# Five plain MLP pairs per layer take their weights' low parts from adding transfers, and a thirteenth pair per layer takes seven products

## The chip, the core and the metric

The kernel runs on one core of a Trainium2 chip. The core has TensorE (PE in the profile; its weight loads, which run beside its matmuls, are PEld), VectorE (DVE), ScalarE (ACT), GpSimd (POOL) and SyncE (SP), and 16 DMA engines that move data between HBM and SBUF. Each engine runs its own instructions in a fixed order and waits at semaphores for the others. The metric is the time of one execution on the device, in microseconds (us).

## The reference, cut to what matters

A decoder trunk of two layers in float32, on 512 positions of width 1024. Each layer has a mixer, a cross-attention into 256 memory tokens, and a gated MLP. The change is in the MLP:

```python
def conv_ffn(h, w_up, w_conv, w_down):
    u = causal_dwconv(h @ w_up, w_conv)
    gate, val = jnp.split(u, 2, axis=-1)
    return (jax.nn.silu(gate) * val) @ w_down
...
for l in range(DEPTH):
    ...
    x = x + conv_ffn(rmsnorm(x, norm_ffn[l]), ffn_w_up[l], ffn_conv[l], ffn_w_down[l])
```

`w_up` is 1024 x 5632 and `w_down` 2816 x 1024, so a layer has 22 pairs of 128-wide columns of `w_up`: gate column block j and value block 22+j.

## The kernel before

**Two parts per operand.** Each float32 operand is carried as two parts in TensorE's reduced float32 type: `hi`, the rounded value, and `lo`, what is left of it. A product is three matmuls: hi with hi, hi with lo, lo with hi (L484). Activations lie transposed, with features on partitions and the 512 positions as columns.

**Weights.** All weights lie in HBM as `wts`, in slots of 128 x 1024 float32 (512 KB). SP loads slot after slot into a ring of three buffers, `raw` (the function `loads`). The function `prep` makes `hi` by a cast on ACT (L431) and `lo` by a subtraction raw - hi on DVE (L446), each in a ring of five buffers, and then frees the raw buffer. A plain up-projection pair has two slots (four of the eight k blocks each) and 8 x 2 x 3 = 48 matmuls of 512 columns, in `lin_stream`.

**Pairs with seven products.** The pairs in the table `SEVEN` take another way, with matrices halved in each direction (2 x 2 blocks) and seven block products in place of eight. `prep_halved` takes the two slots as four blocks of 128 x 512, splits the first slot ("a") and one block ("d") as they are, makes sums and differences of the blocks in place (four DVE operations of 128 x 512), and splits these two slots ("b" and "c"). `lin_halved` runs the products, each four k steps of three matmuls 256 wide, and puts them together by seven additions 256 wide on DVE. What the products read of the activations is made once per layer by `fold`: scaled rows (`N["S"]`, tiles `y` and `h`) and their differences and sums (`N["T"]`, tiles `kl`, `pt`, `so`, `rrow`), four steps of two feature blocks; a product waits for the step that it reads. Before, pairs 8 to 11, 13 and 15 to 21 are in the table, in both layers.

**Order in the MLP.** `FFN_ORDER` sets it: up-projections 0 to 7, then the first part of the down-projection (columns in four pieces, `d 0 0` to `d 0 3`) with pairs 8 to 10 between the pieces, then pairs 11 to 16, the second part with 17 to 20 between, pair 21, and the rest of the down-projection. The MLP's norm runs beside the first pairs: sums of squares (`nacc`, `sq`) are turned by PE, reduced by DVE, POOL takes the power -1/2 (tile `k`, L446, from `s` and `mhalf`), PE spreads that over the partitions (`tr<-ident,k`, L488), and ACT copies it into the tile `rrow`. Pairs 0 to 5 run on unscaled rows `hs`, and their results are multiplied by `rrow` afterwards; pairs 6 and 7 and all later ones read rows that are scaled already.

**What sets the order.** No engine's order is written by hand. Streams of operations (loads, preparation, each matmul stream, each epilogue) ask the class `Issue` for buffers and for their turn. It keeps a modelled time for every engine, takes the operation that can start first, and among those within a small tolerance the one of lowest priority number. So a change in one stream's operations or modelled times can move others. The chip then runs each engine's list in that order, whatever the true times are.

## Time and profile before

| | |
|---|---|
| runs, median (lowest to highest) of 3 | 1478.06 us (1477.45 to 1478.25) |
| the profiled execution, its time | 1477.59 us |
| its span | 1475.8 us |
| granted clock of TensorE, mean | 1.00 |
| PE busy | 1469.9 us, 7832 matmuls |
| weight loads busy | 1265.6 us |
| DVE busy | 1165.7 us (79% of the span) |
| ACT busy | 784.1 us (53%) |
| POOL busy | 65.9 us (4%) |
| read from HBM | 142.92 MB |

The profile is taken from one execution. Its time contains its span and a little around it. A row of the costliest groups reads: line, engine, operation, output and inputs by the program's names with their tile sizes, how often, then busy time, the mean of one in ns, and the idle time just before them with what ended most of it. A row of the trace by time reads: start, length, engine, line, operation. The arrow `<-` behind a wait names the engine, tile and line whose work ended it. The clock is 1.00 throughout, so a matmul's time is the same in every stage.

### The profile page before, as it was taken

What the parts mean: (1) busy time and instruction counts of PE and PEld (TensorE: products, weight loads), DVE (VectorE), ACT (ScalarE), POOL (GpSimd) and SP (SyncE); (2) the same over time, 40 slices, a digit from 0 to 9 for tenths busy, and PEclk for the clock granted to TensorE, in tenths of its full rate; (3) what the DMA queues carried; (4) which work ended last, traced back from release to release, by engine and by line L of the source; (5) the groups of instructions that cost most, each with busy time, mean ns of one, the idle gap of its engine ahead of it and who ended that gap; (6) DMA issues with size and microseconds to landing.
All of it is one profiled execution on the core that took longest, in us unless ns stands there. A gap on an engine that the chain in (4) does not pass through costs nothing.

```text
span 1475.8 us, 20602 instructions
## 1 busy us (share of the span) xinstructions
PE 1469.9 (100%) x7832; PEld 1265.6 (86%) x7832; DVE 1165.7 (79%) x1953; ACT 784.1 (53%) x1297; POOL 65.9 (4%) x139
## 2 busy tenths in 40 slices
PE   9999999999999999999999999999999999999998
PEld 8888888888888899999888888888888889989897
DVE  7689767665898888988688989867657998788883
ACT  6576446453654445445477877755435654354441
POOL 3210000000000000000100000000000000000000
PEclk9999999999999999999999999999999999999999
DMA  6122435311232221324221121451212222323232
GB/s 237 58 86 72 138 134 173 113 58 58 100 107 94 98 93 68 114 98 139 94 72 58 58 100 58 143 171 66 86 64 101 100 75 100 112 86 104 96 113 74
DMA packets 42721, 146.33 MB, mean 99 GB/s; under 512 B 4864, under 2 KB 5376, under 8 KB 42624
## 3 DMA queue, kind: packets, MB, share of 16 engines
q1 hardware_dynamic: 42624, 145.04, 28.8%
q8 instruction: 61, 1.00, 0.3%
q14 instruction: 36, 0.29, 0.1%
HBM read 142.92 MB, written 2.10 MB: 98 GB/s over the span
## 4 chain that ended last, share of the span: by engine, by line
PE 96%; DVE 2%; ACT 1%; issue 0%; DVEq 0%; POOL 0%; POOLq 0%
PE acc L484 72%; PE sc L484 11%; PE pv L484 6%; PE tr L484 5%; PE tr L488 3%; ACT h L431 0%; DVE lo L446 0%; ACT g L434 0%; DVE h L446 0%; DVE c L446 0%; DVE g L446 0%; DVE g L1545 0%; DVE kl L454 0%; ACT pt L431 0%; DVE pt L446 0%
## 5 line engine op out<-in xcount | busy, mean ns | idle before, releaser
L484 PE MATMUL acc<-hs,hi 128*128 128x512 f32 x1568 | 495.2, 392 | 0.0
L431 ACT CAST hi<-raw 128x1024 fp32r<-128x1024 f32 (+1 forms) x288 | 297.4, 1039 | 220.2 <-PE acc L484 81.2
L446 DVE TENSOR_TENSOR lo<-raw,hi 128x1024 fp32r<-128x1024 f32 (+1 forms) x288 | 345.4, 1206 | 67.0 <-ACT hi L431 64.6
L484 PEld LDWEIGHTS acc<-hs,hi 128*128 128x128 f32 x1568 | 292.8, 188 | 57.7
L484 PE MATMUL acc<-hs,lo 128*128 128x512 f32 x784 | 307.0, 392 | 0.0
L484 PE MATMUL acc<-h,hi 128*128 128x512 f32 (+1 forms) x672 | 195.6, 375 | 0.0
L484 PE MATMUL acc<-hi,hs 128*128 128x512 f32 x544 | 176.2, 395 | 0.0
L484 PEld LDWEIGHTS acc<-hs,lo 128*128 128x128 f32 x784 | 147.3, 188 | 28.6
L484 PEld LDWEIGHTS acc<-h,hi 128*128 128x128 f32 x672 | 122.4, 188 | 22.4 <-DVE x L446 0.6
L446 DVE TENSOR_TENSOR x<-x,acc 128x512 f32<-128x512 f32 (+1 forms) x105 | 70.9, 680 | 71.3 <-PE acc L484 71.0
L484 PE MATMUL acc<-h,lo 128*128 128x512 f32 (+1 forms) x336 | 124.8, 374 | 0.0
L484 PEld LDWEIGHTS acc<-hi,hs 128*128 128x128 f32 x544 | 101.3, 188 | 19.8 <-ACT hs L434 0.2
L484 PE MATMUL acc<-lo,hs 128*128 128x512 f32 x272 | 106.4, 392 | 0.0
L454 DVE SCALAR_TENSOR_TENSOR g<-c,pp,g 128x510 f32<-128x510 f32 (+1 forms) x144 | 101.5, 747 | 0.9 <-ACT g L434 0.9
L484 PE MATMUL acc<-y,hi 128*128 128x512 f32 (+1 forms) x352 | 99.2, 363 | 0.0
L484 PEld LDWEIGHTS acc<-h,lo 128*128 128x128 f32 x336 | 63.3, 188 | 11.3
L484 PEld LDWEIGHTS acc<-y,hi 128*128 128x128 f32 x352 | 63.6, 189 | 10.6
L446 DVE TENSOR_TENSOR g<-g,g 128x512 f32<-128x512 f32 (+2 forms) x112 | 62.9, 569 | 4.2 <-ACT g L434 1.7
L434 ACT ACTIVATE g<-c,pp 128x512 f32<-128x512 f32 x72 | 49.5, 719 | 30.4 <-DVE c L446 30.2
L434 ACT ACTIVATE g<-sc,rq 128x128 f32<-128x128 f32 (+7 forms) x128 | 62.0, 540 | 3.6 <-PE sc L484 3.3
L484 PE MATMUL acc<-y,lo 128*128 128x512 f32 (+1 forms) x176 | 63.7, 362 | 0.0
L431 ACT CAST pt<-tr 128x128 fp32r<-128x128 f32 (+2 forms) x96 | 43.0, 456 | 31.1 <-PE tr L488 30.6
(238 smaller groups left out, 2432.4 us busy)
## 6 DMA issues: line engine op xcount, KB each, us to landing
raw<-wts SPq DMA_DIRECT2D x256, 512.0 KB, 3.7
x<-xT SPq DMA_DIRECT2D x16, 256.0 KB, 5.4
raw<-wts SPq DMA_DIRECT2D x8, 256.0 KB, 5.3
raw<-memT SPq DMA_DIRECT2D x4, 512.0 KB, 4.4
outT<-x SPq DMA_DIRECT2D x7, 256.0 KB, 2.0
outT<-x SPq DMA_DIRECT2D x2, 128.0 KB, 1.7
pp<-par SPq DMA_DIRECT2D x1, 175.5 KB, 4.9
sq<-par SPq DMA_DIRECT2D x1, 128.0 KB, 5.1
```

The source lines that it names most:

```text
L431: return nc.scalar.copy(out=out.ap, in_=in_.ap)
L434: return nc.scalar.activation(out=out.ap, in_=in_.ap, func=func, scale=_raw(scale), **kw)
L446: lambda: _ve(eng).tensor_tensor(out=out.ap, in0=in0.ap, in1=in1.ap, op=op))
L454: lambda: nc.vector.scalar_tensor_tensor(out=out.ap, in0=in0.ap, scalar=_raw(scalar), in1=in1.ap, op0=op0, op1=op1))
L484: lambda: nc.tensor.matmul(out.ap, lhsT.ap, rhs.ap, start=start, stop=stop))
L488: return Op("PE", 0.109, [in_, ident_v], [out], lambda: nc.tensor.transpose(out.ap, in_.ap, ident_v.ap))
```

## The change

Three edits go together.

1. **A thirteenth pair with seven products.** Pair 7 joins the table `SEVEN` in both layers. It was the last plain pair ahead of the first down-projection; it now runs 84 matmuls 256 wide in place of 48 that are 512 wide.
2. **Low parts by adding transfers.** For pairs 2 to 6 of both layers (the set `LOW`, two slots each, 20 slots in all) DVE's subtraction goes. ACT writes minus the rounded raw value into `lo` (an ACTIVATE with scale -1), and a transfer that POOL issues adds the slot from HBM onto it: `lo` = wts - hi. The planner takes 1.0 us of POOL for the issue and counts the result as there 10 us later (`land`).
3. **Another layout and other signs in the halved pairs.** Their four blocks are stored one behind the other in HBM, in the order a11, a21, a22, a12 by block row and column, and a load takes two of them (rows of 2 KB in place of 4 KB). Some of the sums change sign: three of the four operations in `prep_halved` become additions, and three of the additions in `lin_halved` become subtractions.

The file also gains a path in which sums of blocks are made in HBM (`sums_in_dram`, `SUMMED`, `ADDED`, `LOW7`); its tables are empty, so nothing of it runs. `FFN_ORDER` is written out with the same content.

```diff
-SEVEN = {l: (8, 9, 10, 11, 13, 15, 16, 17, 18, 19, 20, 21) for l in range(2)}
+SEVEN = {0: (7, 8, 9, 10, 11, 13, 15, 16, 17, 18, 19, 20, 21), 1: (7, 8, 9, 10, 11, 13, 15, 16, 17, 18, 19, 20, 21)}
+
+SUMMED = {0: {}, 1: {}}
...
+LOW = {GN[n] for n in ('U2_0', 'U2_1', 'U3_0', 'U3_1', 'U4_0', 'U4_1', 'U5_0', 'U5_1', 'U6_0', 'U6_1')}
+LOW7 = {GN[n] for n in ()}
...
             self.free_at[op.eng] = end
+            end += op.land
...
+    def add_dma(out, in_):
+
+        out = vw(out)
+        i = in_.ap if isinstance(in_, V) else in_
+        o = Op("POOL", 1.0, [out] + [x for x in (in_,) if isinstance(x, V)], [out],
+               lambda: nc.gpsimd.dma_start(out=out.ap, in_=i, accum_op=ALU.add, max_dma_last_dim=2048))
+        o.land = 10.0
+        return o
...
+    def blocks(gi):
+
+        return wts[FIRST[gi]:FIRST[gi] + 2].rearrange("s p c -> (s p c)").rearrange("(b p c) -> b p c", b=4, p=P)
...
+    def halved_loads(gi):
+        x = blocks(gi)
+        take = [("a", x[0:4:3]), ("r", x[1:3])]
...
+        for n, src in take:
+            w = 512 if n == "d" else SLOT
+            raw = yield AL(pRAW, F32, (P, w), parts=w // 512)
+            v = raw.v().re("p (b c) -> p b c", c=512)
+            src = src.re("b p c -> p b c") if isinstance(src, V) else src.rearrange("b p c -> p b c")
+            yield dma(v, src, w)
+            raws[gi, n] = raw
...
     def prep_halved(gi):
...
-        yield tt(a11, a11, a21, ALU.subtract)
+        yield tt(a11, a11, a21, ALU.add)
         yield tt(a21, a21, a22, ALU.add)
-        yield tt(a22, a22, a11, ALU.subtract)
-        yield tt(a12, a12, a22, ALU.subtract)
+        yield tt(a22, a22, a11, ALU.add)
+        yield tt(a12, a12, a22, ALU.add)
...
                     yield act(hi, raw)
-                    yield tt(lo, raw, hi.v().f32(), ALU.subtract)
+                    if gi in LOW:
+                        yield act(lo, raw, scale=-1.0)
+                        yield add_dma(lo, wts[FIRST[gi] + s])
+                    else:
+                        yield tt(lo, raw, hi.v().f32(), ALU.subtract)
                     prepped[gi, s, 0] = prepped[gi, s, 1] = (hi, lo)
                 free(raw)
...
+        def sub(out, a, ps):
+            return tt(out, a, ps[:, :256], ALU.subtract)
+
+        def neg(out, a, ps):
+            return tt(out, ps[:, :256], a, ALU.subtract)
...
-        then(Until(lambda: "p1" in st), add(c12, c11, p6), lambda: free(p6), flag("p6"),
+        then(Until(lambda: "p1" in st), sub(c12, c11, p6), lambda: free(p6), flag("p6"),
...
-             add(c12, c12, p5), flag("p5"), add(c22, c21, p5), lambda: free(p5),
-             add(c21, c21, p4), lambda: free(p4), lambda: done(1, u2))
+             sub(c12, c12, p5), flag("p5"), neg(c22, c21, p5), lambda: free(p5),
+             neg(c21, c21, p4), lambda: free(p4), lambda: done(1, u2))
```

Lines behind the edits shift by 8 (up to 17 further on): DVE's and POOL's L446 is L454 after, ACT's L431 and L434 are L439 and L442, PE's L484 is L492, the new transfer is L508.

What the edits do to the order shows at three places of the first layer; the second layer has the same at its own. On POOL, around the power that gives the MLP norm, this stood before (the rows with `mhalf` are powers; the third is that of the MLP norm):

```order
L446 TENSOR_TENSOR k_3078<-s_3113,mhalf 128x4
L446 TENSOR_TENSOR k_3223<-s_3273,mhalf 128x4
L446 TENSOR_TENSOR k_3722<-s_3743,mhalf 128x4
L446 TENSOR_TENSOR k_7008<-s_7025,mhalf 128x4
L497 MEMSET g_7056 128x512
```

And this after, at the same place:

```order
L454 TENSOR_TENSOR k_3080<-s_3115,mhalf 128x4
L454 TENSOR_TENSOR k_3225<-s_3275,mhalf 128x4
L508 DMA lo_3689<-wts 128x2x512
L508 DMA lo_3716<-wts 128x2x512
L454 TENSOR_TENSOR k_3723<-s_3743,mhalf 128x4
L508 DMA lo_3747<-wts 128x2x512
L508 DMA lo_3826<-wts 128x2x512
L508 DMA lo_3859<-wts 128x2x512
```

Two of the layer's ten adding transfers (pair 2's two slots) stand ahead of the power on POOL, eight behind it. On ACT, from the copy of the norm's row on, as pairs 0 to 2 end (`hi` casts of raw slots, `y` and `h` casts for the fold, `g` activations of the pairs' results), this stood before:

```order
L431 COPY rrow_3768<-tr_3753 128x512
L434 ACTIVATE g_3787<-c_3692,pp 128x512
L434 ACTIVATE g_3793<-c_3738,pp 128x512
L434 ACTIVATE g_3805<-c_3797,pp 128x512
L431 CAST hi_3819<-raw_3703 128x1024
L434 ACT_TABLE_LOAD
L434 ACTIVATE g_3787<-g_3787 128x512
L431 CAST y_3836<-c_3780 128x512
L431 CAST h_3842<-g_3793 128x512
```

And this after, where `lo_3826` and `lo_3859` are the copies for pair 3's second and pair 4's first slot:

```order
L439 CAST hi_3825<-raw_3717 128x1024
L442 ACT_TABLE_LOAD
L442 ACTIVATE g_3791<-g_3791 128x512
L439 CAST y_3840<-c_3784 128x512
L442 ACTIVATE lo_3826<-raw_3717 128x1024
L439 CAST h_3848<-g_3797 128x512
L439 CAST hi_3858<-raw_3738 128x1024
L442 ACTIVATE g_3809<-g_3809 128x512
L442 ACTIVATE g_3863<-c_3850,pp 128x512
L439 CAST y_3875<-c_3785 128x512
L442 ACTIVATE lo_3859<-raw_3738 128x1024
```

Each cast of a `hi` is followed, some rows later, by the new copy into `lo` from the same raw buffer, with rows of the fold and of the epilogues between them. The third place is the end of the fold on DVE, with pair 7 beside it. Before, from the last four sums of the fold (`c`) on to its last two low parts (`pt_3777` and `rrow_3779`):

```order
L446 TENSOR_TENSOR c_4256<-c_4256 128x256
L446 TENSOR_TENSOR c_4256<-c_4257,c_4256 128x256
L446 TENSOR_TENSOR c_4257<-c_4257,c_4256 128x256
L446 TENSOR_TENSOR c_4257<-c_4257 128x256
L446 TENSOR_TENSOR pt_3777<-c_4256,pt_3777 128x512
L454 SCALAR_TENSOR_TENSOR g_4311<-acc_4130,pp,g_4311 128x511
L446 TENSOR_TENSOR rrow_3779<-c_4257,pt_3777 128x512
```

And the rows from the second of those sums on after, where `raw_4045` and `raw_4084` are pair 7's two loads:

```order
L454 TENSOR_TENSOR c_4187<-c_4188,c_4187 128x256
L454 TENSOR_TENSOR raw_4045<-raw_4045,raw_4084 128x512
L462 SCALAR_TENSOR_TENSOR g_4242<-c_4235,pp,g_4242 128x511
L454 TENSOR_TENSOR c_4188<-c_4188,c_4187 128x256
L454 TENSOR_TENSOR raw_4084<-raw_4084 128x512
L462 SCALAR_TENSOR_TENSOR g_4242<-c_4235,pp,g_4242 128x510
L454 TENSOR_TENSOR c_4188<-c_4188 128x256
L454 TENSOR_TENSOR pt_3781<-c_4187,pt_3781 128x512
L454 TENSOR_TENSOR g_4242<-g_4242,g_4197 128x512
L454 TENSOR_TENSOR raw_4084<-raw_4084,raw_4045 128x512
L462 SCALAR_TENSOR_TENSOR g_4275<-acc_4153,pp,g_4275 128x511
```

Three of pair 7's four sums now stand among the last steps of the fold; its last low part (`rrow_3783`) comes three rows further on, ahead of the fourth sum. On PE, pair 7's seven products stand where its wide matmuls stood, ahead of the first down-projection, and the rows outside the MLPs keep their order but for single matmuls of the norms.

## The prediction

> **What bounds the kernel now.** I read the page first, for the chain that ended last and TensorE's (PE's) share of it.

> ```profile
> span 1475.8 us, 20602 instructions
> ...
> PE 96%; DVE 2%; ACT 1%; issue 0%; DVEq 0%; POOL 0%; POOLq 0%
> ```

> PE carries 96% of the chain. What VectorE (DVE) or ScalarE (ACT) save counts only where PE waits for them, so the waits by engine come second; for PE they are these, in the whole run.

> ```profile
> PE pv L484 <- POOL pt L497: 1.1, 1, 1.1
> PE sc L484 <- DVE s L1022: 0.4, 1, 0.4
> PE sc L484 <- ACT g L434: 0.3, 1, 0.3
> ```

> None lies in the MLPs. The windows third: the plain up-projections of the first MLP, the rest of it, and the second MLP's plain part.

> ```profile
> 389.00:474.00 85.00, 85.00 (x382) 70.59 (x381) 80.72 (x123) 47.49 (x67) 0.00 (x0) 1.00 0.26 89
> ...
> 475.00:738.00 263.00, 263.00 (x1630) 237.73 (x1630) 216.11 (x327) 120.65 (x160) 4.32 (x11) 1.00 0.30 101
> ...
> 1133.00:1218.00 85.00, 85.00 (x379) 70.34 (x378) 79.48 (x121) 46.83 (x67) 0.94 (x1) 1.00 0.26 88
> ```

> The columns are the stretch, its length, then busy time of PE, weight loads, DVE, ACT and GpSimd (POOL). PE is busy all the time at clock 1.00; DVE is near full in the plain parts (80.7 of 85 us) and hides behind PE. So the MLPs cost what PE's matmuls cost at their pitch, and a busy DVE costs nothing yet.

> **PE's own work.** The chain in order of time (start, length, what) gives the pitch.

> ```profile
> 344.91 39.44 PE acc L484 x174
> ...
> 474.25 1.44 PE sc L484 x12
> 475.69 1.44 PE pv L484 x12
> ```

> The first row is 512-wide matmuls alone: 39.44/174 = 226.7 ns each. The others are one product of a seven-product pair each: 12 matmuls, 256 wide, 120.0 ns each. Pair 7 in each layer leaves 2 column blocks x 8 k x 3 = 48 wide matmuls, 10.88 us, for 7 x 12 = 84 narrow ones, 10.08 us. That saves 0.80 us a pair, **1.60 us** in both layers. Everything else that PE runs stays the same.

> [...]

> **DVE and ACT.** These groups hold the kinds of operation that change; the last two figures ahead of the idle time are busy us and mean ns of one.

> ```profile
> L446 DVE TENSOR_TENSOR lo<-raw,hi 128x1024 fp32r<-128x1024 f32 x280 | 339.9, 1221 | 61.1 <-ACT hi L431 58.8
> ...
> L431 ACT CAST hi<-raw 128x1024 fp32r<-128x1024 f32 x280 | 292.5, 1052 | 217.2 <-PE acc L484 81.2 <-DVE raw L446 62.3 <-DMA raw<-wts 56.5
> ...
> L446 DVE TENSOR_TENSOR raw<-raw,raw 128x512 f32<-128x512 f32 x72 | 49.5, 687 | 0.6
> ...
> L446 DVE TENSOR_TENSOR c<-c,sc 128x256 f32<-128x256 f32 x96 | 37.1, 416 | 0.2
> ```

> Ten low parts of a layer leave DVE: 10 x 1.22 = 12.2 us. Pair 7 gives up two (2.4 us) and takes three whole ones, a half-size one and four sums at 0.69, and seven 256-wide additions at 0.42: 3.7 + 3.4 + 2.9 = 10.0 us. DVE nets about 4.6 us less a layer. The negated copy on ACT isn't in the trace; I take the cast of its size, so ACT gains 10 x 1.05 = 10.5 us a layer, and some 2 for pair 7, on 47.5 busy in 85. Bounds for a changed sign or a swapped operand are the rows themselves, which hold adds and subtractions of one size. All of this lies beside PE, so I cost it at nothing.

> What pair 7 could uncover is the fold: its products read the folded activations, which are finished last here.

> ```profile
> 454.30 0.68 DVE L446 TENSOR_TENSOR rrow<-c,pt 128x512 fp32r<-128x512 f32 x1
> ...
> L446 DVE TENSOR_TENSOR lo<-raw,hi 128x1024 fp32r<-128x1024 f32 x11 | 13.5, 1230 | 0.0
> ...
> 461.78 0.61 PE L484 MATMUL acc<-h,hi 128*128 128x512 f32 x2
> ```

> The middle row counts low parts from 389.2 to 455. By the new order one of that size, a half-size one and three sums of pair 7 are left ahead of the last fold: 10 x 1.23 go, 4 x 0.69 come, and the fold ends some 9 us earlier, near 445. The last row is the first down-projection, so pair 7 takes PE's 10.88 us ahead of it, from 450.9, and its third product ends its reads of the fold at 455. The cover is about 9 us; without it PE would wait for what is missing of it.

> **The halved pairs' loads** stay 512 KB each, in rows half as long.

> ```profile
> raw<-wts SPq DMA_DIRECT2D x256, 512.0 KB, 3.7
> ...
> DMA to landing us min/median/max: 3.3/3.7/6.1
> ...
> 465.82 1.22 DVE L446 TENSOR_TENSOR lo<-raw,hi 128x1024 fp32r<-128x1024 f32 x1
> ...
> 477.21 0.28 PE L484 MATMUL tr<-kl,lo 128*128 128x256 f32 x1
> ```

> The bounds are 3.3 and 6.1 us to landing, so a load can come 2.4 us later or 0.4 earlier; the last two rows show such a pair's low part made 10 us before PE reads it. Cost nothing; without that cover, up to 2.4 us a pair.

> **The adding transfers.** Two questions: how long POOL is held, and when the sum has landed.

> POOL first. The new order puts two transfers ahead of the power that gives the MLP's norm.

> ```profile
> 381.90 1.05 ACT L431 CAST hi<-raw 128x1024 fp32r<-128x1024 f32 x1 [0.90 <-PE acc L484]
> ...
> 385.81 1.01 POOL L446 TENSOR_TENSOR k<-s,mhalf 128x4 f32<-128x4 f32 x1 [59.48 <-DVE s L464]
> 388.08 0.60 PE L488 MATMUL tr<-ident,k 128*128 128x128 f32 x4
> ...
> L493 SPq DMA_DIRECT2D raw<-wts x264: 327/328/714, 1.2 to 1439.2; - x132
> ...
> L446 POOL TENSOR_TENSOR s<-s,mhalf 128x8 f32<-128x8 f32 x8 | 14.1, 1758 | 55.8 <-DVE s L469 35.0 <-DVE s L464 19.0 <-DVE s L446 1.7
> ```

> The second transfer waits for cast and copy of pair 2's second half: 381.90 + 2 x 1.05, so POOL issues it at about 384.2. PE transposes the power's result at 388.08, one matmul earlier in the new order, 387.85; the power takes 1.01 us, so it must start by 386.8. Behind it queue PE's transposes, ACT's row copy and DVE's first scalings, which free PE's accumulators. An issue may hold POOL for up to 2.6 us before PE waits. Bounds for one: 0.33 us (SyncE's) and 1.76 us (POOL's longest row); I take 1.0, the power's own. No wait at either end.

> [...]

> Then the landing. Of the ten low parts the tightest is the second of pair 3, the next the second of pair 4.

> ```profile
> 393.75 1.06 ACT L431 CAST hi<-raw 128x1024 fp32r<-128x1024 f32 x1 [1.04 <-PE acc L484]
> ...
> 396.66 0.60 ACT L431 CAST y<-c 128x512 fp32r<-128x512 f32 x1
> ...
> 404.77 1.05 ACT L431 CAST hi<-raw 128x1024 fp32r<-128x1024 f32 x1
> ...
> 410.55 0.39 PE L484 MATMUL acc<-hs,lo 128*128 128x512 f32 x1
> ...
> 421.43 0.39 PE L484 MATMUL acc<-hs,lo 128*128 128x512 f32 x1
> ```

> Pair 3's copy stands behind the cast at 396.66 in ACT's new order (its high part is cast at 393.75) and ends at about 397.25 + 1.0 = 398.3; PE reads it at 410.55: 12.3 us. Pair 4's cast is at 404.77, one 0.6 us cast and the copy follow, to 407.5; PE reads at 421.43: 13.9 us. Bounds for issue and landing: 3.3 us, the quickest load, and 2 x 6.1 + 1.76 = 14.0, since what lies there is read as well as what is added. I take 2 x 3.7 + 1.0 = 8.4, nearest the median load: nothing waits. At 14.0 PE waits 1.7 + 0.1 us a layer, 3.6 in all. What hides the transfers is the ring of five buffers; without it each would cost its 8.4 us.

> **The sum.** -1.60 on PE, and nothing else. The profiled execution took 1477.59 us, its span and 1.8 around it: 1475.99. It stands 0.47 below the median of the runs, 1478.06, so I forecast **1476.4**.

> **The rivals.**
> - Slower: the sums land late. It decides where landing takes over 12.3 us; from 13.1 it has eaten the gain (2 x 0.8). With four median loads' time and the issue, 15.8 us, PE waits 3.5 and 1.9 us a layer, 10.8 in all: 1487.3. For it: nothing in this trace adds in a transfer, and each element is read twice and written. Against it: loads of that size take 3.7 us, with the transfer engines a quarter busy (0.26 above).
> - POOL is held too long: at twice its longest row, 3.5 us, the power starts 0.9 us late, and PE with it, in both layers: 1478.2. For it, the queue above; against it, every row of POOL is under 1.8 us.
> - Pair 7's results are late: they come out of seven products and a chain of additions, and the first down-projection needs them. By the order its last k stands behind a product and a half of pair 8, about 2 us. If they miss by 2 us, or the fold does, it is 4 us: 1480.4.
> - The change doesn't do what it says: pair 7's 84 matmuls run no faster than 48 wide ones. The rows of the other pairs speak against it: 1478.1.

> **How the numbers follow.** A measurement of this kernel can tell about 0.2%, 3.0 us, from no change: 1475.1 to 1481.0. Forecast 0.60, late sums 0.17, POOL 0.11, pair 7 0.07, no saving 0.05. The forecast alone lies within the spread of the runs (0.8 us), 1475.6 to 1477.2. The range goes down to 1475.2, the lowest run less 1.6 and most of that spread, and up over both upper bounds together (1476.4 + 3.6 + 1.8) and the spread to 1483; most of the late sums, 0.1, and a few hundredths of the others are left out. No case gives 3 us; I leave 0.04 for faster. Of the late sums and pair 7, 0.16 are beyond 1481.

> **What would show it.** Right: PE's count 7904 (72 more), no PE wait for `lo` on a transfer nor for POOL's `k`, chain 96% PE, DVE busy some 9 us less, ACT some 25 more; pair 7 as seven rows of 1.44 us. Wrong: a wait of PE for a transfer into `lo` (late sums), PE's transposes behind POOL (held queue), or a gap ahead of pair 7's third product or in the first down-projection.

## The result and the profile after

| | median us | lowest to highest | ratio to before, 95% interval |
|---|---|---|---|
| before | 1478.15 | 1477.45 to 1478.39 | |
| changed | 1491.71 | 1490.78 to 1492.68 | 1.0092 [1.0079, 1.0104] |

The changed kernel is 13.6 us slower. The forecast was 1476.4, the range ended at 1483.0. The profiled execution took 1492.37 us. Its page begins so, and gives the chain that ended last like this:

```profile
span 1490.6 us, 20821 instructions
## 1 busy us (share of the span) xinstructions
PE 1474.7 (99%) x7904; PEld 1270.9 (85%) x7904; DVE 1157.7 (78%) x1959; ACT 805.1 (54%) x1323; POOL 90.4 (6%) x159
...
PE 90%; issue 4%; DVE 2%; ACT 2%; DMA 1%; POOL 1%; SPq 0%; DVEq 0%; POOLq 0%; ACTq 0%
```

The work is what was forecast: 7904 matmuls, DVE 8.0 us less (forecast 9), ACT 21 us more (forecast 25). But PE no longer carries 96% of the chain. The waits of PE name what does:

```profile
PE tr L496 <- POOL k L454: 8.7, 2, 4.4
PE acc L492 <- DMA lo<-wts: 1.4, 3, 0.8
PE pv L492 <- POOL pt L514: 1.1, 1, 1.1
```

The first row wasn't there before. Once in each layer PE's transposes wait 4.4 us for POOL's power `k`, the place of the rival "POOL is held too long". The second row is the rival "the sums land late", three times and briefly. Next stands the first of the long waits, as the trace by time shows it: POOL's rows first, then ACT's, DVE's and PE's.

```profile
381.14 1.42 POOL L508 DMA_DIRECT2D lo<-wts  x1 [54.41 <-ACT lo L442]
390.34 1.22 POOL L508 DMA_DIRECT2D lo<-wts  x1 [7.78 <-issue]
391.10 1.52 POOL L454 TENSOR_TENSOR k<-s,mhalf 128x4 f32<-128x4 f32 x1
396.35 1.24 POOL L508 DMA_DIRECT2D lo<-wts  x1 [3.72 <-ACT g L442]
```

```profile
383.15 1.06 ACT L442 ACTIVATE lo<-raw 128x1024 fp32r<-128x1024 f32 x1
...
386.33 1.06 ACT L442 ACTIVATE lo<-raw 128x1024 fp32r<-128x1024 f32 x1
```

```profile
385.63 0.17 DVE L472 TENSOR_SCALAR s<-k 128x4 f32<-128x4 f32 x1
394.45 1.29 DVE L454 TENSOR_TENSOR c<-acc,rrow 128x512 f32<-128x512 f32 x2 [8.65 <-ACT rrow L439]
```

```profile
387.92 0.39 PE L492 MATMUL acc<-hs,lo 128*128 128x512 f32 x1
392.68 1.11 PE L496 MATMUL tr<-ident,k 128*128 128x128 f32 x4 [4.37 <-POOL k L454]
393.44 1.20 PE L492 MATMUL acc<-hs,hi 128*128 128x512 f32 x2
394.44 0.63 PE L492 MATMUL acc<-hs,lo 128*128 128x512 f32 x1
394.87 0.63 PE L492 MATMUL acc<-hs,hi 128*128 128x512 f32 x1
```

Read them in this order. The copy that pair 2's second transfer needs ends at 383.15 + 1.06 = 384.2, as forecast. The power's operand is there at 385.8. Yet POOL issues that transfer only at 390.34, and the profile finds nothing it waited for ("issue"). The power stands behind it and starts at 391.10 instead of by 386.8; PE's last matmul ahead of the transposes started at 387.92. In the packet records of the trace the first transfer's last packet ends at 389.77, 0.57 us before the second issue. The third, whose copy ended at 387.4, is issued at 396.35; the second one's last packet ended at 395.80. The packet records of all 20 transfers show the same: this kernel never has two adding transfers under way.

DVE is idle from 385.8 to 394.45 in these rows, so work on DVE isn't what holds POOL here.

Behind the wait there is a second loss. PE's matmuls of 512 columns start 0.43 us apart (394.44 to 394.87), not 0.227. The windows of 388 to 393 and 393 to 398 us show the granted clock, the third figure from the end. After, then before:

```profile
388.00:393.00 5.00, 0.63 (x4) 0.32 (x3) 0.00 (x0) 0.00 (x0) 2.29 (x2) 0.81 0.63 184
393.00:398.00 5.00, 5.00 (x15) 4.02 (x14) 1.95 (x3) 1.92 (x3) 1.24 (x1) 0.51 0.53 90
```

```profile
388.00:393.00 5.00, 5.00 (x26) 4.13 (x24) 3.67 (x6) 2.65 (x4) 0.00 (x0) 1.00 0.29 108
393.00:398.00 5.00, 5.00 (x24) 4.14 (x23) 4.13 (x7) 3.97 (x5) 0.00 (x0) 1.00 0.00 0
```

Fifteen matmuls in 5 us instead of 24, at half the clock. Windows cut at the change of clock show when it fell and when it came back:

```profile
388.00:391.10 3.10, 0.31 (x2) 0.00 (x0) 0.00 (x0) 0.00 (x0) 0.76 (x1) 1.00 0.79 274
391.10:397.90 6.80, 5.22 (x15) 4.25 (x16) 1.95 (x3) 1.92 (x3) 2.76 (x3) 0.50 0.50 77
397.90:400.00 2.10, 2.10 (x11) 1.72 (x10) 1.44 (x3) 0.72 (x1) 0.00 (x0) 1.00 0.80 96
```

The clock fell within the wait, 2.8 us after the end of PE's last matmul (387.92 + 0.39), and came back 5.2 us after PE took up work again (392.68). From the starts of PE's matmuls, what each gap has over its pitch (227 ns for 512 columns, 120 for 256, 60 for a transpose), less what before has at the same places, sums up to:

| | us over the pitch |
|---|---|
| the waits for POOL's `k`, 4.53 and 4.49 | 9.0 |
| the slow matmuls behind them, 2.5 and 2.7 | 5.2 |
| three waits for a sum, with what follows each | 2.2 |
| pair 7's saving, as forecast | -1.6 |
| sum | 14.8 |

The spans differ by 1490.6 - 1475.8 = 14.8 us.

### The profile page after: what moved, and what is told of

Read it like the earlier page. It is cut to its first block, busy times and chain, and to the rows that moved or that the text cites. A ratio compares the mean times of both kernels' runs of the same rounds, so it can differ in the third digit from the quotient of the medians.

```text
span 1490.6 us, 20821 instructions
## 1 busy us (share of the span) xinstructions
PE 1474.7 (99%) x7904; PEld 1270.9 (85%) x7904; DVE 1157.7 (78%) x1959; ACT 805.1 (54%) x1323; POOL 90.4 (6%) x159
## 3 DMA queue, kind: packets, MB, share of 16 engines
q0 software_dynamic: 5440, 10.49, 4.5%
## 4 chain that ended last, share of the span: by engine, by line
PE 90%; issue 4%; DVE 2%; ACT 2%; DMA 1%; POOL 1%; SPq 0%; DVEq 0%; POOLq 0%; ACTq 0%
PE acc L492 65%; PE sc L492 12%; PE pv L492 6%; PE tr L492 5%; PE tr L496 3%; DMA lo<-wts 1%; POOL lo L508 1%; DVE lo L454 0%; ACT h L439 0%; ACT g L442 0%; DVE c L454 0%; DMA x<-xT 0%; DVE g L454 0%; DVE h L454 0%; DVE g L1619 0%
## 5 line engine op out<-in xcount | busy, mean ns | idle before, releaser
L492 PE MATMUL acc<-hs,hi 128*128 128x512 f32 x1568 | 498.0, 394 | 0.0
L439 ACT CAST hi<-raw 128x1024 fp32r<-128x1024 f32 (+1 forms) x290 | 299.0, 1039 | 204.8 <-DMA raw<-wts 72.9
L454 DVE TENSOR_TENSOR lo<-raw,hi 128x1024 fp32r<-128x1024 f32 (+1 forms) x270 | 323.3, 1204 | 59.9 <-ACT hi L439 56.0
L492 PEld LDWEIGHTS acc<-hs,hi 128*128 128x128 f32 x1568 | 294.6, 189 | 58.1
L492 PE MATMUL acc<-hs,lo 128*128 128x512 f32 x784 | 308.7, 394 | 0.3 <-DMA lo<-wts 0.3
L492 PE MATMUL acc<-h,hi 128*128 128x512 f32 (+1 forms) x648 | 187.5, 373 | 0.0
L492 PE MATMUL acc<-hi,hs 128*128 128x512 f32 x544 | 176.2, 395 | 0.3 <-ACT hs L442 0.3
L492 PEld LDWEIGHTS acc<-hs,lo 128*128 128x128 f32 x784 | 148.4, 189 | 29.7 <-DMA lo<-wts 0.7
L492 PEld LDWEIGHTS acc<-h,hi 128*128 128x128 f32 x648 | 117.5, 189 | 21.1 <-DVE x L454 0.6
L454 DVE TENSOR_TENSOR x<-x,acc 128x512 f32<-128x512 f32 (+1 forms) x105 | 70.7, 679 | 69.9 <-PE acc L492 69.5
L492 PE MATMUL acc<-h,lo 128*128 128x512 f32 (+1 forms) x324 | 120.0, 373 | 1.1 <-DMA lo<-wts 1.1
L492 PEld LDWEIGHTS acc<-hi,hs 128*128 128x128 f32 x544 | 101.3, 188 | 20.1 <-ACT hs L442 0.5
L462 DVE SCALAR_TENSOR_TENSOR g<-c,pp,g 128x510 f32<-128x510 f32 (+1 forms) x152 | 106.7, 744 | 3.4 <-ACT g L442 3.3
L492 PE MATMUL acc<-lo,hs 128*128 128x512 f32 x272 | 106.4, 392 | 0.0
L492 PE MATMUL acc<-y,hi 128*128 128x512 f32 (+1 forms) x328 | 90.9, 358 | 0.0
L442 ACT ACTIVATE g<-c,pp 128x512 f32<-128x512 f32 x76 | 52.1, 718 | 47.9 <-DVE c L454 47.9
L492 PEld LDWEIGHTS acc<-h,lo 128*128 128x128 f32 x324 | 61.0, 188 | 12.7 <-DMA lo<-wts 1.9
L492 PEld LDWEIGHTS acc<-y,hi 128*128 128x128 f32 x328 | 59.0, 189 | 9.5
L454 DVE TENSOR_TENSOR g<-g,g 128x512 f32<-128x512 f32 (+2 forms) x112 | 62.7, 568 | 4.3 <-ACT g L442 1.8
L442 ACT ACTIVATE g<-sc,rq 128x128 f32<-128x128 f32 (+7 forms) x128 | 62.0, 540 | 3.6 <-PE sc L492 3.3
L492 PEld LDWEIGHTS acc<-lo,hs 128*128 128x128 f32 x272 | 51.1, 188 | 9.8
L439 ACT CAST pt<-tr 128x128 fp32r<-128x128 f32 (+2 forms) x96 | 43.0, 456 | 29.9 <-PE tr L496 29.3
## 6 DMA issues: line engine op xcount, KB each, us to landing
raw<-wts SPq DMA_DIRECT2D x256, 512.0 KB, 3.8
lo<-wts POOLq DMA_DIRECT2D x20, 512.0 KB, 5.8
raw<-memT SPq DMA_DIRECT2D x4, 512.0 KB, 4.2
```

Source lines behind the costliest of these rows:

```text
L439: return nc.scalar.copy(out=out.ap, in_=in_.ap)
L442: return nc.scalar.activation(out=out.ap, in_=in_.ap, func=func, scale=_raw(scale), **kw)
L454: lambda: _ve(eng).tensor_tensor(out=out.ap, in0=in0.ap, in1=in1.ap, op=op))
L462: lambda: nc.vector.scalar_tensor_tensor(out=out.ap, in0=in0.ap, scalar=_raw(scalar), in1=in1.ap, op0=op0, op1=op1))
L492: lambda: nc.tensor.matmul(out.ap, lhsT.ap, rhs.ap, start=start, stop=stop))
```

## The experiments

Two theories for the late issue. R: a POOL transfer needs room for its descriptors in what the program sets aside (`dynamic_dma_scratch_size`, 1024 bytes in this kernel, as before the change), an adding transfer of 256 rows fills over half of it, and the next must wait until it has left. S: POOL has one adding transfer under way at a time, whatever the room. That it is descriptors that fill the room is the author's assumption; no trace shows them. The kernels with 1216 bytes of room, with longer rows, with no transfer ahead of the power, and with pair 7 but no transfers ran beside 27 runs of before with a median of 1478.26, the other four beside 27 with 1478.40. The changed kernel itself did not run again beside them; its 1491.71 was measured beside a before of 1478.15.

**More room.** Nothing else changes; the order of all instructions is the same.

```diff
-    nc = bacc.Bacc("TRN2", target_bir_lowering=False, num_devices=1, dynamic_dma_scratch_size=1024)
+    nc = bacc.Bacc("TRN2", target_bir_lowering=False, num_devices=1, dynamic_dma_scratch_size=1216)
```

> [...] Theory R: an adding transfer of 256 rows fills the old room so far that the next can't be issued until it has left; with more room pair 2's second transfer issues when its copy is made (near 384.3 us of the span), the norm's power follows by 386.8, PE's two waits of 4.5 us and the slow clock behind them (2.6 us each) go: 1476.0 to 1478.2. Theory S: POOL has one adding transfer under way at a time, whatever the room: 1490.8 to 1492.7, as the changed kernel.

Measured: 1476.14 us (1475.79 to 1477.85), ratio 0.9986 [0.9978, 0.9995]. POOL's rows at the same place:

```profile
381.36 1.41 POOL L508 DMA_DIRECT2D lo<-wts  x1 [54.59 <-ACT lo L442]
384.63 1.20 POOL L508 DMA_DIRECT2D lo<-wts  x1 [1.87 <-ACT lo L442]
386.01 1.03 POOL L454 TENSOR_TENSOR k<-s,mhalf 128x4 f32<-128x4 f32 x1 [0.18 <-DVE s L472]
391.38 1.25 POOL L508 DMA_DIRECT2D lo<-wts  x1 [4.35 <-ACT g L442]
```

The second transfer is issued when its copy is made, and the power waits for DVE alone, as the prediction had it. The third still has to wait, though only for the first: it is issued at 391.38, and the packet records end the first transfer at 390.80. Two fit now, not three. R holds, S falls.

**A smaller step of room**, 1088 bytes. If two transfers fit, the time is that of 1216 bytes, 1476.1; if not, that of the changed kernel, 1490.8 to 1492.7.

> [...]

Measured: 1476.09 us (1475.68 to 1476.44), ratio 0.9982 [0.9973, 0.9991]. POOL's second and third transfer:

```profile
384.60 1.20 POOL L508 DMA_DIRECT2D lo<-wts  x1 [1.98 <-ACT lo L442]
...
390.43 1.25 POOL L508 DMA_DIRECT2D lo<-wts  x1 [3.43 <-ACT rrow L439]
```

The second is issued when its copy is made, the third waits for the first, whose last packet ends at 389.84. So 64 bytes decide over 15.6 us: the size that is set aside decides whether the next transfer can be issued. Two transfers don't fit into 1024 bytes (second issue at 390.34), and they do into 1088 (384.60). If a room may be filled to its last byte, one takes more than 512 and at most 544 bytes, an estimate from these two runs.

**Longer rows**, with the room as in the changed kernel.

```diff
-               lambda: nc.gpsimd.dma_start(out=out.ap, in_=i, accum_op=ALU.add, max_dma_last_dim=2048))
+               lambda: nc.gpsimd.dma_start(out=out.ap, in_=i, accum_op=ALU.add, max_dma_last_dim=4096))
```

> The changed kernel with the adding transfers in rows of 4096 in place of 2048 bytes, so 128 rows in place of 256 a transfer, room as it was. Theory R: half the descriptors, so two or three transfers fit and the second is issued when its copy is made: 1476.0 to 1478.2. Theory S: 1490.8 to 1492.7, and issues still about 6 us apart wherever they queue.

Measured: 1475.90 us (1475.64 to 1476.75), ratio 0.9984 [0.9975, 0.9992]: the change as it was meant, faster than before and than the changed kernel, and 0.1 us below the range that was expected.

```profile
381.08 1.07 POOL L508 DMA_DIRECT2D lo<-wts  x1 [54.57 <-ACT lo L442]
384.40 0.86 POOL L508 DMA_DIRECT2D lo<-wts  x1 [2.25 <-ACT lo L442]
385.77 1.03 POOL L454 TENSOR_TENSOR k<-s,mhalf 128x4 f32<-128x4 f32 x1 [0.50 <-DVE s L472]
387.56 0.92 POOL L508 DMA_DIRECT2D lo<-wts  x1 [0.76 <-ACT lo L442]
```

The profile pages count 144 packets a transfer here (2880 for 20), where the changed kernel has 272 (5440). Now three transfers are under way: the third is issued at 387.56, while the first one's last packet ends at 389.68. An issue also holds POOL for less, 0.9 us in place of 1.2.

**No transfer ahead of the power.** Pair 2 goes back to DVE, so all adding transfers stand behind the power.

```diff
-LOW = {GN[n] for n in ('U2_0', 'U2_1', 'U3_0', 'U3_1', 'U4_0', 'U4_1', 'U5_0', 'U5_1', 'U6_0', 'U6_1')}
+LOW = {GN[n] for n in ('U3_0', 'U3_1', 'U4_0', 'U4_1', 'U5_0', 'U5_1', 'U6_0', 'U6_1')}
```

> The changed kernel without pair 2's adding transfers (its low parts are DVE's again); eight a layer stay, all behind the norm's power on POOL. Both theories: the power waits for no transfer, so 14.2 us go. R and S: the first of pair 3 can issue from 387.4, nine us earlier than in the changed kernel, so the later ones are on time as well: 1476.0 to 1477.0. If the waits at the norm had another cause than the place of the transfers on POOL: above 1485.

Measured: 1476.68 us (1475.92 to 1477.45), ratio 0.9989 [0.9980, 0.9998]. PE has no wait for POOL's `k`. One kind of wait stays:

```profile
PE acc L492 <- DMA lo<-wts: 0.8, 2, 0.4
```

The time is in the range, but the expectation's word that the later transfers are on time did not hold. With one transfer at a time, each about 6 us (median landing 5.8 in the changed kernel), the last of a layer still come a little late; without pair 2's there are eight to run through and not ten.

**PE kept busy in the wait.** The changed kernel, with 32 matmuls that do nothing useful in front of the transposes.

```diff
+FILL = 32
...
             ps = yield AL(aTR)
+            if N["g"].startswith("norm_ffn"):
+                z = N["A"][0][0].v()
+                for _ in range(FILL):
+                    o = mm(ps[:, :256], z[:, :P], z[:, :256], True, True)
+                    o.reads.append(r[:, :NB])
+                    yield o
             yield from row_of(ps, r)
```

> The changed kernel with 32 more matmuls of 256 columns (120 ns each, 3.84 us; their results are overwritten) on PE in each layer, right ahead of the transposes that wait for the norm's power; the wait for POOL stays. If it is PE's idling that lowers its clock afterwards: the idle time shrinks from 4.5 to about 0.7 us, the matmuls behind it run at 227 ns, and 2.6 us a layer go: 1486.5 (1485.5 to 1487.5). If the slow matmuls behind the wait have another cause (the transfers that run at that time): about 1491.7, with matmuls of 430 ns behind the wait as before.

Measured: 1484.16 us (1483.63 to 1487.69), ratio 1.0042 [1.0027, 1.0058]: 7.5 us faster than the changed kernel, with 64 matmuls more. POOL's second issue, PE's rows, and the window of the wait:

```profile
389.11 1.22 POOL L510 DMA_DIRECT2D lo<-wts  x1 [6.74 <-issue]
```

```profile
388.21 3.99 PE L494 MATMUL tr<-hs 128*128 128x256 f32 x32
392.04 0.60 PE L498 MATMUL tr<-ident,k 128*128 128x128 f32 x4
392.39 0.70 PE L494 MATMUL acc<-hs,hi 128*128 128x512 f32 x2
392.94 0.40 PE L494 MATMUL acc<-hs,lo 128*128 128x512 f32 x1
393.17 0.62 PE L494 MATMUL acc<-hs,hi 128*128 128x512 f32 x2
```

```profile
388.00:393.00 5.00, 5.00 (x41) 4.88 (x40) 0.00 (x0) 0.33 (x1) 2.29 (x2) 1.00 0.87 202
```

The pitch behind the transposes is 0.23 us at once (392.94 to 393.17) and the clock stays at 1.00, though POOL's second issue still waits for the first transfer (389.11, where its copy is made near 384) and the DMA engines are busier than in the changed kernel (the last figure but one, 0.87, there 0.63). So it is PE's idling that lowered the clock, not the transfers beside it. The time came out 1.3 us below the range that was expected: the power starts 1.2 us earlier than in the changed kernel, so the 32 matmuls cover the whole wait, and the waits for late sums shrink from 1.4 to 0.2 us. The time fits the longer rows' 1475.9 plus 2 x 3.84 = 1483.6.

**Pair 7 without the transfers.**

```diff
-LOW = {GN[n] for n in ('U2_0', 'U2_1', 'U3_0', 'U3_1', 'U4_0', 'U4_1', 'U5_0', 'U5_1', 'U6_0', 'U6_1')}
+LOW = set()
```

> The changed kernel with no adding transfer: pair 7 with seven products, the layout and the signs of the halved pairs stay. If the saving of pair 7 is the 0.80 us a layer of the prediction and DVE covers its sums: 1476.4 (1475.6 to 1477.2). If DVE, which has its ten low parts a layer back, is late with the fold or with pair 7's parts: 1478 to 1484, with PE waits ahead of pair 7's products.

Measured: 1484.76 us (1483.20 to 1486.55), ratio 1.0043 [1.0030, 1.0057]: the second branch, 0.8 us beyond its end. PE's waits are at pair 7's third product:

```profile
455.37 0.28 PE L492 MATMUL pv<-pt,sq 128*128 128x256 f32 x1
457.04 0.38 PE L492 MATMUL pv<-pt,sq 128*128 128x256 f32 x1 [1.39 <-ACT pt L439]
458.27 0.58 PE L492 MATMUL pv<-rrow,sq 128*128 128x256 f32 x1 [0.84 <-DVE rrow L454]
458.65 0.42 PE L492 MATMUL pv<-pt,sq 128*128 128x256 f32 x1
458.86 0.41 PE L492 MATMUL tr<-kl,hi 128*128 128x256 f32 x1
```

PE waits first for a high part of the fold from ACT, then for its last low part, which DVE has ready at 458.2, over two us after PE would have come to it. The matmuls behind run at half pace here too (0.21 us apart in place of 0.12):

```profile
454.30:457.70 3.40, 1.73 (x13) 1.33 (x11) 3.40 (x7) 1.83 (x5) 0.00 (x0) 1.00 0.49 154
457.70:461.10 3.40, 2.83 (x13) 2.83 (x14) 3.40 (x5) 2.46 (x3) 0.00 (x0) 0.51 0.05 8
```

The clock fell at 457.7, during the second wait, with PE busy for 1.73 of the 3.40 us before. The adding transfers are what makes room on DVE for pair 7: between this kernel and the one with longer rows lie 8.9 us.

**The transfers without pair 7**, in longer rows, and **the layout alone** (no transfers). Both have the old table of pairs, as the diff shows; the first also has the 4096 of the longer rows, the second `LOW = set()`.

```diff
-SEVEN = {0: (7, 8, 9, 10, 11, 13, 15, 16, 17, 18, 19, 20, 21), 1: (7, 8, 9, 10, 11, 13, 15, 16, 17, 18, 19, 20, 21)}
+SEVEN = {0: (8, 9, 10, 11, 13, 15, 16, 17, 18, 19, 20, 21), 1: (8, 9, 10, 11, 13, 15, 16, 17, 18, 19, 20, 21)}
```

> The adding transfers in rows of 4096 bytes with the old table of pairs (pair 7 plain). Theory: by themselves they only free DVE, which PE doesn't wait for here: 1478.3 (1477.3 to 1479.0), no PE wait at the norm; what rows4k gained (1475.9) is then all pair 7's. If the transfers give something of their own: below 1477.3.

Measured: 1477.65 us (1477.42 to 1478.62), ratio 0.9995 [0.9986, 1.0004].

> The changed kernel with the old table of pairs and without adding transfers: only the new layout, loads and signs of the halved pairs are left. If they cost nothing, as predicted: 1478.3 (1477.3 to 1479.0). If loads in rows of 2048 bytes come late or the swapped subtractions cost DVE time that PE waits for: over 1479.5.

Measured: 1477.98 us (1477.45 to 1480.24), ratio 0.9998 [0.9989, 1.0007]. Neither can be told from before, as expected. Pair 7 beside the transfers is then worth 1477.65 - 1475.90 = 1.75 us; the two ran beside different runs of before, whose medians differ by 0.14, so about 1.6.

## Why the prediction was wrong

- **The step that failed** is POOL's hold: "Bounds for one: 0.33 us (SyncE's) and 1.76 us (POOL's longest row); I take 1.0, the power's own." One issue does take 1.2 to 1.4 us, within the bounds. But the prediction took the issues to be independent of each other. In the changed kernel the second can't be issued until the first transfer has left, and it held POOL from 384.2 to 390.3, 6.1 us. The sum for the landing, "2 x 3.7 + 1.0 = 8.4", was the term that belonged here: it is nearly what the first transfer took (8.6 us from issue to last packet), and it was used only for the reader of the sum, not for what queues behind the next transfer. Nothing in the profile of before could show the room's size; the code did, in its 1024 bytes.
- **The rival "POOL is held too long"** had the place, the queue behind it and the 2.6 us of slack right. Its price was 0.9 us a layer, from twice POOL's longest row; the trace shows 4.5.
- **What a wait of PE costs** was counted as the wait alone. Here 4.5 us of idling cost 2.5 to 2.7 us more in slow matmuls; the run with filled waits, where the clock stays at 1.00, shows that it is the idling. In the changed kernel the clock fell to 0.50 after 2.8 us of idling and came back after 5.2 us of work; in pair 7's run without transfers it fell to 0.51 with no wait longer than 1.39 us. How busy PE must be to keep its clock, no run here measures.
- **The sums land late**: the landing itself lay within its bounds. The row of the changed kernel's transfers gives it:

```profile
DMA to landing us min/median/max: 5.6/5.8/8.9
```

  Within the forecast's 3.3 to 14.0, with 8.4 taken. The two loads' time in these terms stands for reading what lies there as well as what is added; no run shows a second read, and the page counts the data of the 20 transfers once (10.49 MB). The late sums (2.2 us in all) come from the queue, one transfer of some 6 us at a time while PE uses up a slot in 5.4, and not from the landing; with room for two or three under way they vanish, though the longer rows' median landing is 8.0 us. The prices of this rival add a wait at pair 4 to one at pair 3, though a wait at pair 3 also puts off the read of pair 4; by its own numbers 14.0 us would cost 3.4 and 15.8 us 7.0 in all, not 3.6 and 10.8.
- **Pair 7** was right in kind and size: 1.60 forecast, 1.6 to 1.75 measured, its products are rows of 1.44 us, and its results come in time. The kernel with longer rows has these in its chain:

```profile
454.11 1.44 PE pv L492 x12
455.55 1.44 PE tr L492 x12
```

- **The fold's cover** was right in its sign and too large. Its last low part ends at 449.7 in that kernel:

```profile
449.02 0.69 DVE L454 TENSOR_TENSOR rrow<-c,pt 128x512 fp32r<-128x512 f32 x1
```

  That is 5.6 us ahead of the product's last reads, where 9 were forecast. Without the transfers it ends at 458.2, and PE waits, as "without it PE would wait for what is missing of it" said.
- **The layout, the signs, DVE's and ACT's work** cost nothing that can be told from before, as forecast: the layout and signs alone gave 1477.98, the transfers with ACT's copies 1477.65. (In `lin_halved` four additions became subtractions, not three as the section on the change says.)

With room for two transfers the time is 1476.1 (1088 or 1216 bytes), with longer rows 1475.9, against the 1476.4 forecast. So the error is the one hold, the clock behind it, and the late sums of the same queue.

## What to carry to other kernels

- A transfer that an engine issues is an instruction in that engine's order. Ask not only how long its issue takes, but what it may have to wait for (room, the transfer before it), and then what stands behind it: here an issue that came at 390.34 in place of 384.2 put the power off to 391.10 and PE's transposes by 4.4 us. An operation that PE needs belongs ahead of it; with no transfer ahead of the power the time was 1476.68.
- Where transfers that POOL issues wait for one another, try more room and longer rows; here half as many rows (1475.90 us), or 64 bytes more (1476.09 us), turned 0.92% slower into 0.16 and 0.18% faster.
- Price a wait of PE of several us with the slow matmuls behind it: here, with waits of 4.5 us, the two together came to 1.6 times the wait.
